# Local attention: the high and low parts of the values side by side in one operand

## The chip, the cores and the metric

The kernel runs on one core of a Trainium2 chip. The metric is the time of one execution on the device in microseconds (us); a version is told by the median of several executions. One execution of each version was also taken by the hardware profiler. The engines of the core are PE (matrix products; PEld is its loading of weights), DVE (vector engine), ACT (scalar engine), POOL (a further engine for elementwise work) and SP, which here issues the transfers (DMA).

## The reference, cut to what matters

The whole is one layer of a hybrid encoder on 1024 tokens of 1024 features, in single precision: a mixer in which windowed softmax attention and a gated DeltaNet run side by side, a cross-attention into 256 memory tokens, and a SwiGLU network. The change touches the last step of the windowed attention (8 query heads in 2 groups, 64 features a head, windows of 128 queries that see up to 384 keys):

```python
def _window_attention(q, k, v, sink):
    ...
    p = jnp.exp(scores - m)
    denom = jnp.sum(p, axis=-1, keepdims=True) + jnp.exp(sk - m)
    o = jnp.einsum('bnhgqk,bnkhd->bnqhgd', p / denom, vw)
    return o.reshape(b, s, ATTN_WIDTH)
```

## The kernel before

PE takes its operands as a short form of float32 (fp32r in the profile). To keep the precision, the kernel writes an operand as a high part, the rounded value, and a low part, what is left (the helper `split`: a copy on ACT at line 102, a subtraction on DVE at line 103). A product of two such operands is taken as three: high by high, high by low and low by high, added up in one PSUM bank.

The attention works in 16 windows: 8 blocks of 128 tokens by 2 groups of heads. `window(n, g)` is a generator with one `yield`. Its first half loads keys (`kr`, line 610), queries (`qr`, line 611) and values (`vr`, line 613), splits them, takes the scores (line 633) and the softmax (lines 635 to 650). Its second half turns the softmax weights of each block of 128 keys by four transposes on PE (line 656), splits them into `ph` and `pl`, and multiplies them by the values (line 661) into the one PSUM tile `po` (named `pow` in the profile, one buffer). There are 3 blocks in a window, 2 at the two ends of the sequence: 44 blocks in all. The values have only 64 features, so the kernel writes each of them twice side by side (`v2`), which fills the 128 columns of the weights and gives the same sums in both halves of the partitions of `po`. Two copies on ACT (lines 664 and 665) take the even heads from the lower half and the odd ones from the upper half into `ao` (one buffer), and a transfer (line 666) stores it in `d_mix`, where the output projection (`mid_gemm`, line 991) reads it later.

`next_windows` starts a window and then finishes the one started before. The written order (`ORDER_2`, `ORDER_3`) mixes these calls with the projections of queries, the levels of the DeltaNet's triangular inverses (lines 569 and 575), the scan of the DeltaNet (line 763, with updates on DVE at lines 784 and 804) and the projections of the memory tokens (lines 891 and 907). The order in which each engine gets its instructions, the queue of SP with its transfers among them, is then set by a scheduler that works from a timeline of its own, so a change in one place can move instructions in others. Each engine works its instructions off in that order.

Of the kernel before, what the change touches and what calls it, by code (L numbers as in the profile page):

```python
# [10 lines left out]
F32 = mybir.dt.float32  # L11
F32R = mybir.dt.float32r
I32 = mybir.dt.int32
AF = mybir.ActivationFunctionType
ALU = mybir.AluOpType
# [4 lines left out]
P = 128  # L20
# [55 lines left out]
def tile_hybrid_block(  # L76
# [6 lines left out]
    nc = tc.nc  # L83
# [9 lines left out]
    def f32(ap):  # L93
        return ap.bitcast(F32)

    def bc(ap, axis, shape):
        return ap.unsqueeze(axis).to_broadcast(list(shape))

    def split(hi, lo, src, scale=None, eng=None):

        if scale is None:
            nc.scalar.copy(hi, src)  # L102
            (eng or nc.vector).tensor_tensor(lo, src, f32(hi), ALU.subtract)  # L103
        else:
            nc.scalar.activation(hi, src, AF.Identity, scale=scale)
            nc.vector.scalar_tensor_tensor(lo, src, scale, f32(hi), ALU.mult, ALU.subtract)

    def pool(name, bufs, **kw):
        return tc.tile_pool(name=name, bufs=bufs, reuse_waits="tile", **kw)
# [73 lines left out]
    d_mix = dram.tile([D, S], F32, name="d_mix")  # L183
# [26 lines left out]
    for hf in range(2):  # L210
        hi = hx.tile([P, KT, HALF], F32R, name=f"hhi{hf}")
        lo = hx.tile([P, KT, HALF], F32R, name=f"hlo{hf}")
        for j in range(4):
            t = 4 * hf + j
# [95 lines left out]
    for hf in range(2):  # L310
        pp = pg.tile([P, 512], F32, tag="pg", name="pg")
        for k in range(KT):
            for a in range(2):
                nc.tensor.matmul(pp, wabr[:, k, :], hT[hf][a][:, k, :], start=(k == 0 and a == 0),
                                 stop=(k == KT - 1 and a == 1))
# [282 lines left out]
    def window(n, g):  # L598

        tok = slice(n * P, (n + 1) * P)  # L600
        k0, k1 = max(n - 1, 0), min(n + 1, NT - 1) + 1
        nb = k1 - k0
        w = nb * P
        band = C[:, _AT["band0"] - C0 + (k0 - n + 1) * P:][:, 0:w]


        kr = tw.tile([P, 384], F32, tag="kr", name="kr", bufs=1)[:, 0:w]
        qr = tw.tile([P, 4, P], F32, tag="qr", name="qr", bufs=1)
        for r in range(2):
            nc.sync.dma_start(kr[64 * r:64 * r + 64], d_k[64 * g:64 * g + 64, k0 * P:k1 * P])  # L610
            nc.sync.dma_start(qr[64 * r:64 * r + 64], d_q[256 * g:256 * g + 256, tok].rearrange("(h e) t -> e h t", h=4))
        vr = tw.tile([P, 3, 64], F32, tag="vr", name="vr", bufs=1)[:, 0:nb]
        nc.sync.dma_start(vr, d_v[k0:k1, :, 64 * g:64 * g + 64].rearrange("c p e -> p c e"))
        khi = tw.tile([P, 384], F32R, tag="khi", name="khi")[:, 0:w]
        klo = tw.tile([P, 384], F32R, tag="klo", name="klo", bufs=1)[:, 0:w]
        nc.scalar.copy(khi, kr)
        nc.gpsimd.tensor_tensor(klo, kr, f32(khi), ALU.subtract)
        vhi = tw.tile([P, 3, 2, 64], F32R, tag="vhi", name="vhi")[:, 0:nb]
        vlo = tw.tile([P, 3, 2, 64], F32R, tag="vlo", name="vlo")[:, 0:nb]
        v2 = bc(vr, 2, (P, nb, 2, 64))  # L620
        nc.scalar.copy(vhi, v2)
        nc.gpsimd.tensor_tensor(vlo, v2, f32(vhi), ALU.subtract)
        qs = tw.tile([P, 4, P], F32R, tag="qs", name="qs")
        nc.scalar.copy(qs, qr)
        nc.gpsimd.tensor_tensor(qs[64:128], qr[64:128], f32(qs[64:128]), ALU.subtract)

        m4 = tw.tile([P, 4], F32, tag="m4", name="m4")
        ssum = tw.tile([P, 4], F32, tag="ssum", name="ssum")
        pr = []
        for hh in range(4):  # L630
            pp = pw.tile([P, 512], F32, tag="pw", name="psw")
            for i, kk in enumerate((khi, klo)):
                nc.tensor.matmul(pp[:, 0:w], qs[:, hh, :], kk, start=(i == 0), stop=(i == 1))
            sc = tw.tile([P, 384], F32, tag="sc", name="sc", bufs=8)
            nc.vector.tensor_tensor_reduce(out=sc[:, 0:w], in0=pp[:, 0:w], in1=band, scale=0.125,
                                           scalar=sink[:, 4 * g + hh:4 * g + hh + 1], op0=ALU.add, op1=ALU.max,
                                           accum_out=m4[:, hh:hh + 1])
            pr.append(sc)
        nm = tw.tile([P, 4], F32, tag="nm", name="nm")
        nc.vector.tensor_scalar(nm, m4, -1.0, None, ALU.mult)  # L640
        for hh in range(4):
            nc.scalar.activation(pr[hh][:, 0:w], pr[hh][:, 0:w], AF.Exp, bias=nm[:, hh:hh + 1],
                                 accum_out=ssum[:, hh:hh + 1])
        es = tw.tile([P, 4], F32, tag="es", name="es")
        nc.gpsimd.tensor_tensor(es, sink[:, 4 * g:4 * g + 4], m4, ALU.subtract)
        nc.scalar.activation(es, es, AF.Exp)
        nc.vector.tensor_tensor(es, es, ssum, ALU.add)
        nc.vector.reciprocal(es, es)
        for hh in range(4):
            nc.scalar.mul(pr[hh][:, 0:w], pr[hh][:, 0:w], es[:, hh:hh + 1])  # L650
        yield
        po = pw.tile([P, 4, P], F32, tag="pow", name="pow", bufs=1)
        for j in range(nb):
            pp = pw.tile([P, 512], F32, tag="pw", name="ptw")
            for hh in range(4):
                nc.tensor.transpose(pp[:, hh * P:(hh + 1) * P], pr[hh][:, j * P:(j + 1) * P], ident)
            ph = tw.tile([P, 512], F32R, tag="ph", name="ph")
            pl = tw.tile([P, 512], F32R, tag="pl", name="pl")
            split(ph, pl, pp)
            for i, (vv, pe_) in enumerate(((vhi, ph), (vhi, pl), (vlo, ph))):  # L660
                nc.tensor.matmul(po.rearrange("p h t -> p (h t)"), vv[:, j].rearrange("p r e -> p (r e)"), pe_,
                                 start=(j == 0 and i == 0), stop=(j == nb - 1 and i == 2))
        ao = tw.tile([P, 2, P], F32, tag="ao", name="ao", bufs=1)
        nc.scalar.copy(ao[0:64], po[0:64, 0:4:2, :])
        nc.scalar.copy(ao[64:128], po[64:128, 1:4:2, :])
        nc.sync.dma_start(d_mix[g * 256:(g + 1) * 256, tok].rearrange("(k p) t -> p k t", p=P), ao)

    def next_windows():

        for _ in range(2):  # L670
            last = wins[-1] if wins else None
            if wins_done[0] < 2 * NT:
                wins.append(window(wins_done[0] % NT, wins_done[0] // NT))
                next(wins[-1])
            wins_done[0] += 1
            if last:
                next(last, None)
# [20 lines left out]
    tw = p12.enter_context(pool("tw", 2))  # L698
# [621 lines left out]
    for t in range(NT):  # L1320
        tok = slice(t * P, (t + 1) * P)
# [58 lines left out]
```

## Time and profile before

| what | before |
|---|---|
| median of 3 executions | 1625.35 us (1624.68 to 1629.03) |
| the profiled execution | 1627.8 us, its span 1626.1 us |
| mean granted clock of PE | 0.984 |
| PE busy, share of the span | 96% |
| weight loads busy | 80% |
| DVE, ACT, POOL busy | 58%, 46%, 33% |
| the windows' products (line 661) | from 380 to 615 us, 132 matmuls |

A busy share is the share of the span in which the engine worked on at least one instruction; matmuls overlap in it. The time of a group of instructions (busy us, mean ns of one) is followed by the idle time of its engine just before them and what ended it. The chain that ended last is followed back from the last instruction, at each step to what released it. Times within the span count from its first instruction.

### The profile page before, as it was taken

How to read it: one execution, taken by the hardware profiler on the slowest of the kernel's cores; microseconds unless marked ns; L12 is line 12 of the kernel's file. 1: busy time of each engine (PE TensorE's matmuls, PEld its weight loads, DVE VectorE, ACT ScalarE, POOL GpSimd, SP SyncE). 2: the span in 40 equal slices, each digit the busy share in tenths (PEclk: the TensorE clock that was granted, in tenths of full speed). 3: DMA queues.
4: the chain of work that ended last, by engine and by line, in shares of the span. 5: the costliest groups of instructions: out<-in, count | busy, mean ns of one | idle time of the engine just before them, and what ended most of it. 6: DMA issues, size and time to landing. Idle time of an engine off the chain costs nothing.

```text
span 1626.1 us, 21448 instructions
## 1 busy us (share of the span) xinstructions
PE 1554.1 (96%) x7690; PEld 1298.7 (80%) x7690; DVE 940.8 (58%) x1431; ACT 747.7 (46%) x1518; POOL 543.8 (33%) x501
## 2 busy tenths in 40 slices
PE   6999889999899989999999999999999999999997
PEld 5878778888799868788888777788888888888886
DVE  6855986957677864543356467666545544334332
ACT  5556553236858774564436574233233222444211
POOL 2467653334336600253202221343334332321100
PEclk9999999897999999999999999999999999999999
DMA  6134158574999585354223264432322223565451
GB/s 202 41 117 129 46 176 221 140 179 124 312 300 278 179 278 183 130 194 156 66 65 117 90 199 132 130 117 80 95 79 78 89 93 119 197 220 176 141 178 71
DMA packets 267815, 240.47 MB, mean 148 GB/s; under 512 B 43176, under 2 KB 216637, under 8 KB 267709
## 3 DMA queue, kind: packets, MB, share of 16 engines
q1 hardware_dynamic: 267709, 239.11, 47.2%
q8 instruction: 60, 0.98, 0.2%
q14 instruction: 46, 0.38, 0.1%
HBM read 177.69 MB, written 58.75 MB: 145 GB/s over the span
## 4 chain that ended last, share of the span: by engine, by line
PE 67%; DVE 10%; DMA 6%; issue 3%; ACT 3%; POOL 1%; SPq 1%; POOLq 0%; ACTq 0%; DVEq 0%
PE pmg L991 10%; PE pd L1334 8%; PE pd L1310 7%; PE pE L1163 6%; PE pD L1163 6%; PE pA L1163 6%; PE pcq L260 5%; PE pB L1163 3%; PE psc L763 3%; PE pg L260 3%; DVE acc L285 1%; DVE A L512 1%; PE pcs L1072 1%; DVE tmpb L510 1%; PE pco L1098 1%
## 5 line engine op out<-in xcount | busy, mean ns | idle before, releaser
L102 ACT CAST whi<-wraw 128x1024 fp32r<-128x1024 f32 x108 | 113.3, 1050 | 153.7 <-issue 60.0
L103 POOL TENSOR_TENSOR wlo<-wraw,whi 128x1024 fp32r<-128x1024 f32 x48 | 117.9, 2457 | 165.2 <-ACT whi L102 138.2
L260 PE MATMUL pg<-hhi,whi 128*128 128x512 f32 x352 | 143.0, 407 | 0.0
L260 PE MATMUL pg<-hlo,whi 128*128 128x512 f32 x352 | 142.3, 405 | 0.0
L260 PE MATMUL pg<-hhi,wlo 128*128 128x512 f32 x352 | 142.2, 404 | 0.0
L103 DVE TENSOR_TENSOR wlo<-wraw,whi 128x1024 fp32r<-128x1024 f32 x60 | 74.5, 1243 | 82.6 <-ACT whi L102 77.5
L991 PE MATMUL pmg<-whi,b 128*128 128x512 f32 x384 | 118.4, 395 | 2.6 <-ACT whi L102 2.2
L1163 PE MATMUL pA<-s,whi 128*128 128x512 f32 x352 | 109.5, 392 | 1.4 <-ACT m L1180 1.4
L285 DVE SCALAR_TENSOR_TENSOR acc<-cp,cols,acc 128x1024 f32<-128x1024 f32 x48 | 76.0, 1586 | 34.1 <-ACT acc L283 33.5
L991 PEld LDWEIGHTS pmg<-whi,b 128*128 128x128 f32 x384 | 71.2, 188 | 17.9 <-ACT whi L102 2.7
L1240 POOL TENSOR_TENSOR act<-act,up 128x512 f32<-128x512 f32 x33 | 44.3, 1345 | 112.3 <-issue 59.0
L260 PEld LDWEIGHTS pg<-hhi,whi 128*128 128x128 f32 x352 | 68.6, 195 | 13.6 <-ACT hhi L102 0.3
L260 PEld LDWEIGHTS pg<-hhi,wlo 128*128 128x128 f32 x352 | 68.4, 194 | 13.7
L260 PEld LDWEIGHTS pg<-hlo,whi 128*128 128x128 f32 x352 | 68.2, 194 | 13.5
L1163 PEld LDWEIGHTS pA<-s,whi 128*128 128x128 f32 x352 | 65.3, 188 | 15.1 <-ACT m L1180 2.0
L991 PE MATMUL pmg<-wlo,b 128*128 128x512 f32 x192 | 71.4, 392 | 0.0
L1212 POOL TENSOR_TENSOR sr<-wraw 128x512 f32<-128x512 f32 x22 | 28.4, 1291 | 124.8 <-DMA wraw<-in_w_gate_up_dram 118.1
L1163 PE MATMUL pA<-s,wlo 128*128 128x512 f32 x176 | 68.8, 392 | 1.1 <-DVE wlo L103 1.1
L1334 PE MATMUL pd<-wdh,ath 128*128 128x512 f32 x176 | 69.5, 395 | 0.0
L1334 PE MATMUL pd<-wdl,ath 128*128 128x512 f32 x176 | 69.5, 395 | 0.0
L1334 PE MATMUL pd<-wdh,atl 128*128 128x512 f32 x176 | 69.5, 395 | 0.0
L1310 PE MATMUL pd<-dl,whi 128*128 128x512 f32 x176 | 68.5, 389 | 0.0
(387 smaller groups left out, 4177.3 us busy)
## 6 DMA issues: line engine op xcount, KB each, us to landing
wraw<-in_w_gate_up_dram SPq DMA_DIRECT2D x52, 512.0 KB, 4.1
kv<-d_kv SPq DMA_DIRECT2D x32, 512.0 KB, 6.7
wraw<-in_w_in_dram SPq DMA_DIRECT2D x22, 512.0 KB, 4.1
araw<-d_act SPq DMA_DIRECT2D x22, 512.0 KB, 3.3
draw<-in_w_down_dram SPq DMA_DIRECT2D x22, 512.0 KB, 4.7
atr<-d_act SPq DMA_DIRECT2D x16, 704.0 KB, 4.7
d_act<-act SPq DMA_DIRECT2D x40, 256.0 KB, 2.5
d_kv<-kv SPq DMA_DIRECT2D x8, 1024.0 KB, 6.2
```

The costliest lines, as they stand in the source:

```text
L102: nc.scalar.copy(hi, src)
L103: (eng or nc.vector).tensor_tensor(lo, src, f32(hi), ALU.subtract)
L260: nc.tensor.matmul(p_, w[:, k, :], ah[a][:, k, :], start=(k == 0 and i == 0), stop=(k == nk - 1 and i == 2))
L285: nc.vector.scalar_tensor_tensor(acc, cp[:, t:t + S], taps[t], acc, ALU.mult, ALU.add)
L510: nc.vector.tensor_tensor(tv, A[:, j + 1:, j:j + 1].to_broadcast([P, n, j]), A[:, j:j + 1, 0:j].to_broadcast([P, n, j]), ALU.mult)
L763: nc.tensor.matmul(out[:, d, h, :], lt[:, d, h, :], rt[:, d, h, :], start=True, stop=True)
L991: nc.tensor.matmul(pp[t], act[a][:, k, tt], w_[:, kk, :], start=(k == 0 and i == 0), stop=(k == KT - 1 and i == 2))
L1163: nc.tensor.matmul(out_, w[a][:, k, :], xx[b_][:, k, :], start=(start and k == 0 and i == 0), stop=(k == HK - 1 and i == 2), skip_group_ch ...
L1212: nc.gpsimd.tensor_tensor(s[0], b_[:, 0:HK], b_[:, HK:], ALU.add)
L1240: nc.gpsimd.tensor_tensor(o_, o_, up, ALU.mult)
L1310: nc.tensor.matmul(pps[t], a[:, tt], b_, start=(f == 0 and i == 0), stop=(f == NF - 1 and i == 2))
L1334: nc.tensor.matmul(pp, a[:, f - f0], b_[:, f], start=(f == 0 and i == 0), stop=(f == NF - 1 and i == 2))
```

## The change

The low part of the values takes the place of their second copy. One tile `vhl` holds, for each block of keys, 64 columns of the high part and 64 of the low part, and is the weight operand of two products, by `ph` and by `pl`. The lower half of the partitions of `po` then holds the sums with the high parts and the upper half those with the low parts (the product of the two low parts comes in with them). At the end of a window the upper half is copied to `ao` by ACT, for all four heads, and DVE adds the lower half to it; the copy is written twice in the code, the same both times. `ao` has 64 partitions with four heads in place of 128 with two, and the store is written to match.

```diff
-        vhi = tw.tile([P, 3, 2, 64], F32R, tag="vhi", name="vhi")[:, 0:nb]
-        vlo = tw.tile([P, 3, 2, 64], F32R, tag="vlo", name="vlo")[:, 0:nb]
-        v2 = bc(vr, 2, (P, nb, 2, 64))
-        nc.scalar.copy(vhi, v2)
-        nc.gpsimd.tensor_tensor(vlo, v2, f32(vhi), ALU.subtract)
+
+        vhl = tw.tile([P, 3, 2, 64], F32R, tag="vhl", name="vhl")[:, 0:nb]
+        nc.scalar.copy(vhl[:, :, 0], vr)
+        nc.gpsimd.tensor_tensor(vhl[:, :, 1], vr, f32(vhl[:, :, 0]), ALU.subtract)
...
-            for i, (vv, pe_) in enumerate(((vhi, ph), (vhi, pl), (vlo, ph))):
-                nc.tensor.matmul(po.rearrange("p h t -> p (h t)"), vv[:, j].rearrange("p r e -> p (r e)"), pe_,
-                                 start=(j == 0 and i == 0), stop=(j == nb - 1 and i == 2))
-        ao = tw.tile([P, 2, P], F32, tag="ao", name="ao", bufs=1)
-        nc.scalar.copy(ao[0:64], po[0:64, 0:4:2, :])
-        nc.scalar.copy(ao[64:128], po[64:128, 1:4:2, :])
-        nc.sync.dma_start(d_mix[g * 256:(g + 1) * 256, tok].rearrange("(k p) t -> p k t", p=P), ao)
+            for i, pe_ in enumerate((ph, pl)):
+                nc.tensor.matmul(po.rearrange("p h t -> p (h t)"), vhl[:, j].rearrange("p r e -> p (r e)"), pe_,
+                                 start=(j == 0 and i == 0), stop=(j == nb - 1 and i == 1))
+        ao = tw.tile([P, 4, P], F32, tag="ao", name="ao", bufs=1)[0:64]
+        nc.scalar.copy(ao, po[64:128])
+        nc.scalar.copy(ao, po[64:128])
+        nc.vector.tensor_tensor(ao, po[0:64], ao, ALU.add)
+        nc.sync.dma_start(d_mix[g * 256:(g + 1) * 256, tok].rearrange("(h e) t -> e h t", e=64), ao)
```

## The prediction

> **What bounds the kernel now.** I read the page first, then the busy times of the stretch in which the windows of the local attention run, then the groups of instructions there, the waits, and last the chain of waits piece by piece.
>
> ```profile
> span 1626.1 us, 21448 instructions
> PE 1554.1 (96%) x7690; PEld 1298.7 (80%) x7690; DVE 940.8 (58%) x1431; ACT 747.7 (46%) x1518; POOL 543.8 (33%) x501
> ...
> PE 67%; DVE 10%; DMA 6%; issue 3%; ACT 3%; POOL 1%; SPq 1%; POOLq 0%; ACTq 0%; DVEq 0%
> ```
>
> The matrix engine PE is busy 96% of the span and carries 67% of the chain that ended last, so time taken from PE is worth most where nothing else waits. The next rows cut the stretch of the windows into four parts (length, then busy time of PE, weight loads, DVE, ACT, POOL with counts, granted clock, DMA share, GB/s).
>
> ```profile
> 380.00:420.00 40.00, 34.71 (x156) 29.20 (x157) 25.34 (x60) 27.86 (x71) 16.14 (x18) 0.70 0.56 168
> 420.00:540.00 120.00, 113.28 (x888) 107.68 (x887) 89.81 (x250) 84.80 (x228) 58.79 (x59) 1.00 0.97 303
> 540.00:580.00 40.00, 37.85 (x256) 33.76 (x255) 30.89 (x66) 32.67 (x100) 19.55 (x25) 1.00 0.54 154
> 580.00:620.00 40.00, 35.07 (x165) 27.64 (x164) 23.95 (x34) 29.98 (x51) 0.90 (x2) 1.00 0.86 292
> ```
>
> From 420 to 580 us PE is busy 151 of 160 us at full clock, DVE 121 (75%) and ACT 117 (73%). From 380 to 420 us the granted clock is 0.70, so something other than PE sets the pace there; from 420 to 540 us the DMA engines are 0.97 busy as well. The chain pieces (start, length, what) show where PE's work is what counts and where it is not:
>
> ```profile
> 416.37 9.60 DMA kv<-d_kv
> 426.05 7.33 DMA wraw<-in_w_ckv_dram
> ...
> 436.34 0.70 PE pow L661 x3
> ...
> 442.32 0.69 PE pow L661 x3
> ...
> 464.54 4.26 SPq L610
> 468.85 5.23 DMA kr<-d_k
> ...
> 580.61 10.54 DMA wraw<-in_w_ckv_dram
> ```
>
> **What the change removes.** Of the three products per block of 128 keys (high values by high weights, high by low, low by high) one goes. These are the groups of line 661, first for 380 to 620 us, then its last row again for the parts 380 to 420, 420 to 580 and 580 to 620 us (count, then busy us and mean ns).
>
> ```profile
> L661 PE MATMUL pow<-pl,vhi 128*128 128x512 f32 x44 | 21.2, 481 | 3.6 <-DVE pl L103 3.5
> L661 PE MATMUL pow<-ph,vhi 128*128 128x512 f32 x44 | 20.9, 476 | 10.9 <-ACT ph L102 10.4 <-ACT ao L665 0.4
> L661 PE MATMUL pow<-ph,vlo 128*128 128x512 f32 x44 | 18.3, 415 | 0.0
> L661 PEld LDWEIGHTS pow<-ph,vlo 128*128 128x128 f32 x44 | 9.0, 205 | 0.5
> L661 PE MATMUL pow<-ph,vlo 128*128 128x512 f32 x8 | 4.1, 511 | 0.0
> L661 PE MATMUL pow<-ph,vlo 128*128 128x512 f32 x28 | 11.0, 394 | 0.0
> L661 PE MATMUL pow<-ph,vlo 128*128 128x512 f32 x8 | 3.2, 394 | 0.0
> ```
>
> 44 matmuls go, and with them 44 weight loads. What is one worth? Its row says 415 ns, but matmuls overlap: in the chain three of them take 0.69 us (442.32), so one costs 0.23 us of issue. The price of the whole is 44 x 0.23 = 10.1 us, not the 18.3 us of the row. The Trainium skill, "Perfetto Trace Analysis", section Identifying the Most-Contended Engine, says that matmul busy time misleads because the instructions are pipelined, and that weight-load time is the better measure; by that the removed work is the 9.0 us of the weight-load row, so the sum would be 1.1 us smaller. The trace bears the rule out, 0.23 us in the chain against 415 ns in the group.
>
> How much of the 10.1 us counts? 28 of the 44 lie between 420 and 580 us, where PE is nearly always at work: 28 x 0.23 = 6.4 us, taken in full. Eight lie after 580 us: 8 x 0.23 = 1.8 us, of which I take 0.9, since the chain there runs 10.54 us through a weight transfer that no matmul hastens, and PE is busy only 35.07 of 40 us. Eight lie before 420 us, at a clock of 0.70, ahead of the 9.60 us transfer of kv: at most 8 x 0.23 / 0.70 = 2.6 us, and I take 0, because the next stage starts with that transfer. Together 7.3 us, with ends of 0 and 10.8 us (6.4 + 1.8 + 2.6).
>
> **What it adds and moves.** The rows of the same stretch that price it:
>
> ```profile
> L102 ACT CAST ph<-ptw 128x512 fp32r<-128x512 f32 x44 | 25.5, 583 | 2.8 <-PE ptw L656 2.3
> L664 ACT COPY ao<-pow 64x256 f32<-64x256 f32 x16 | 5.8, 362 | 11.5 <-DMA d_mix<-ao 6.9 <-PE pow L661 4.6
> L665 ACT COPY ao<-pow 64x256 f32<-64x256 f32 x16 | 5.9, 367 | 0.2
> L621 ACT CAST vhi<-vr 128x384 fp32r<-128x384 f32 (+1 forms) x14 | 6.8, 487 | 8.3 <-PE pow L661 8.2
> L622 POOL TENSOR_TENSOR vlo<-vr,vhi 128x384 fp32r<-128x384 f32 (+1 forms) x14 | 13.7, 982 | 66.4 <-ACT vhi L621 38.2 <-PE psw L633 15.8 <-PE pck L891 7.4
> L817 DVE TENSOR_TENSOR ol<-ol,psc 128x512 f32<-128x512 f32 x8 | 5.4, 680 | 0.1
> ```
>
> ACT: each of the 16 windows had two copies of 64 x 256 (0.362 + 0.367 us). Now it has two copies of 64 x 512; the diff writes the same copy twice, and the second one adds nothing but time. No copy of that shape is in the trace. Its bounds are 0.365 us, if the length of a row did not count, and 0.583 us, the cast of 512 elements out of the same memory; I take 0.58, because length is what differs between these rows. That is 16 x (1.16 - 0.73) = 6.9 us more. The cast of the values shrinks from 384 to 192 elements a row: from 0.487 to between 0.36 (the 256-element copy) and about 0.30, so 16 x 0.14 = 2.2 us less. ACT gains 4.7 us of work.
>
> DVE: a new addition of 64 x 512 per window, one operand in PSUM, as the 0.680 us of line 817: 16 x 0.68 = 10.9 us more. POOL: the subtraction for the low part halves, 16 x about 0.45 = 7 us less, and worth nothing: POOL sat idle 66.4 us before these very instructions.
>
> What is queued behind this? The tail of a window is last product, copy, copy, addition, store; it takes 2 x 0.58 + 0.68 = 1.84 us in place of 0.73. In the built order the next window's first product into the same PSUM bank stands 4 us of PE work or more behind the last one, once 2 us (estimated at 0.23 us for a product of 512), so the bank is free in time when ACT and DVE are prompt. On ACT the two copies hold up the casts of the transposed weights (ph), and on DVE the addition holds up pl and the scan's own updates. These are the waits of PE that stand there already, and those of the store:
>
> ```profile
> PE pow L661 <- ACT ph L102: 10.4, 8, 2.2
> PE pow L661 <- DVE pl L103: 3.5, 6, 1.1
> ...
> SPq L666 <- ACT ao L665: 15.3, 9, 5.1
> ```
>
> 13.9 us of waiting for 345 us of ACT and DVE work between 380 and 620 us (sums of the four parts) is 4%; by that the 15.6 us added would cost 0.6 us. Work added where an engine is three quarters full costs more than the mean, so I take 2.0 us, with ends of 0 and 15.6. The store of ao moves behind the addition; the queue of SP waited 15.3 us for ao before. In the built order the store now stands behind loads (of vr, d_q, kr) that used to follow it, so these don't wait longer for it; I cost it at 0, and at 16 x 1.1 = 18 us if every window's loads waited. The store's shape changes from 128 partitions of two rows to 64 of four, each run still 128 floats: 0. The built order also differs over the whole stretch and a little in later ones; I cost that at 0 with 4 us to either side, an estimate from the single holes of 4 to 5 us (464.54, 468.85) that one load in another place makes or mends.
>
> Sum: -7.3 + 2.0 = -5.3 us. The profiled execution took 1627.8 us (span 1626.1), so it would be 1622.5; the median of before is 2.45 us below that execution, so the forecast is 1625.35 - 5.3 = **1620.0 us**. What a measurement of this kernel can tell from no change is about 0.3%, 4.9 us; the forecast lies just beyond.
>
> **Rivals.**
> (a) All the PE time comes back and the added work hides. For it: PE is the chain for 67%. Against it: the clock of 0.70 and the two long transfers. Time 1625.35 - 10.1 = 1615.2; chance 0.08.
> (b) The DMA engines set the pace from 420 to 540 us, so PE merely waits for kv, pz and weights in place of multiplying. For it: share 0.97 and 303 GB/s; chain pieces of DMA of 5 to 10 us. Against it: 113.28 of 120 us of PE busy. Then only what lies after 540 us counts, about a quarter of the 6.4 us plus 0.9: -2.5 us, with the 2.0 us added 1625; chance 0.27.
> (c) Slower: the tail of the window becomes the bound. ACT and DVE take their queues in order; if ph and pl of the next window stand right behind the two copies and the addition, each window lengthens by the 1.84 - 0.73 = 1.1 us of tail. In all 16 windows that is 17.8 us, less the 7.3 us that count: +10.5; in two thirds of them +4.5. It decides from the point at which PE's wait for ph and pl, 13.9 us now, passes 21.2 us (13.9 + 7.3). For it: PE holes of 2.2 us before ph exist now. Time 1630 to 1636, 1632 for one number; chance 0.22.
> (d) The clock. In the profile 380 to 420 us ran at 0.70 while PE was busy 34.71 of 40 us, and 420 to 540 us at 1.00 with 113.28 of 120. If fewer matmuls make PE sparse enough for the lower clock in 20 us more, that costs 20 x 0.30 = 6 us and the gain is gone: 1626. Against it: the longest hole of the dense part is short.
>
> ```profile
> 492.99 0.50 PE L661 MATMUL pow<-ph,vhi 128*128 128x512 f32 x1 [2.19 <-ACT ph L102]
> ```
>
> Chance 0.05. The Trainium skill, "TensorE: Matmul & The Clock Gate", section What's actually happening, states that the clock halves after an idle window of about 3.4 us; a hole of 2.19 us is shorter, so by that rule too the clock should stay.
> (e) The change not doing what it says can be left out: the built order holds two products per block.
>
> **Numbers.** Forecast 0.38 and (a) 0.08 are faster, though near the bound of 4.9 us: part of the forecast's mass (0.04) falls inside it, so faster is 0.42. (b), (d) and that part give 0.36 for no change, (c) 0.22 for slower. The range reaches from 1611 (the 10.1 us and 4 us of better order) to 1635 (rival (c) with 3 us of worse order).
>
> **What would show it.** Right: 88 matmuls on pow, three quarters of their gain in 420 to 580 us, the last window's store some 5 us earlier, copies of about 0.58 us and additions of 0.68, PE's waits for ph and pl under 18 us together. Wrong: scan and windows ending no earlier with more DMA pieces in the chain (b); waits of PE for ph, pl or the new ao above 21.2 us (c); a clock under 1.00 after 420 us (d); copies of 0.37 us or an addition far from 0.68 would upset the price.

## The result, and the profile after

The changed kernel takes 1632.41 us (median of 6 runs, 1632.21 to 1637.4) where the kernel before takes 1627.19 us on the same chip. The ratio is 1.0039 with a 95% interval of 1.0021 to 1.0057: slower by 6.3 us (3.4 to 9.3; here and below microseconds are the ratio less one, times 1628; the two medians themselves lie 5.2 us apart). The forecast was 1620.0 us, faster by 5.3.

First the page of the changed kernel: span, busy times, and shares of the chain that ended last.

```profile
span 1630.5 us, 21375 instructions
...
PE 1545.3 (95%) x7646; PEld 1290.9 (79%) x7646; DVE 945.5 (58%) x1447; ACT 751.5 (46%) x1518; POOL 538.3 (33%) x501
...
PE 62%; DVE 9%; DMA 5%; ACT 4%; issue 3%; POOL 1%; SPq 1%; POOLq 0%; ACTq 0%; DVEq 0%
```

PE has 44 matmuls fewer and is busy 8.8 us less (1554.1 before), yet the span is 4.4 us longer. PE's share of the chain fell from 67 to 62%, so time that was PE's work became waiting. The same four stretches as in the prediction (length, busy time of PE, weight loads, DVE, ACT, POOL, granted clock, DMA share, GB/s) show where:

```profile
380.00:420.00 40.00, 31.79 (x171) 26.50 (x172) 29.52 (x75) 32.66 (x83) 15.41 (x20) 0.83 0.63 191
420.00:540.00 120.00, 111.73 (x878) 106.05 (x878) 94.40 (x252) 84.68 (x221) 55.97 (x59) 1.00 0.95 299
540.00:580.00 40.00, 32.95 (x198) 29.32 (x197) 24.62 (x55) 28.01 (x84) 16.36 (x20) 0.91 0.49 140
580.00:620.00 40.00, 34.47 (x157) 26.74 (x156) 25.35 (x43) 31.84 (x59) 2.96 (x5) 0.96 0.75 253
```

From 540 to 580 us every engine is less busy than before (PE 32.95 for 37.85, DVE 24.62 for 30.89, ACT 28.01 for 32.67): something is waited for in turn, and no engine is full. Up to there the changed kernel was ahead: the scan's 493rd product (psc, line 763) starts at 531.0 us where it started at 536.6. Of this lead 2.7 us stand already at the scan's first product (413.7 for 416.3 us), a place that varies from 412.3 to 418.9 us over the profiles of all kernels here. The scan's last product (line 843) starts at 570.6, before at 570.2. So 5.6 us of lead are gone in 40 us. The merge's first product then starts 2.3 us late (611.6 for 609.3), and the transposes behind it 4.3 us late (682.6 for 678.3); from there the distance no longer changes much. The store of the last window, forecast some 5 us earlier, is issued at 628.2 us where it was at 615.8.

The chain pieces of that stretch (start, length, what) show the turn-taking:

```profile
547.71 1.00 POOL klo L617
548.72 0.48 SPq L610
...
549.25 4.56 DMA kr<-d_k
...
553.89 0.47 ACT khi L616
...
554.92 1.98 ACT sc L641 x7
556.90 0.48 ACT vn L793
...
557.42 3.20 PE psc L763 x16
```

The buffer of the keys (`kr`) comes free when POOL has taken the low part of the last keys (`klo`); only then is the next load issued, and it takes 4.56 us. ACT stands at the cast of those keys, and behind it in ACT's queue are the exponentials and a copy for the scan (`vn`), on which PE waits. From 420 to 580 us as a whole ACT stands no longer for the keys than before (13.1 us for 14.0), so this place is an example and not the account.

The groups of the changed lines, 380 to 620 us as in the prediction (count, busy us, mean ns, then idle time of the engine before them and what ended it):

```profile
L660 PE MATMUL pow<-ph,vhl 128*128 128x512 f32 x42 | 19.6, 466 | 5.8 <-ACT ph L102 4.7 <-DVE ao L665 1.2
L660 PE MATMUL pow<-pl,vhl 128*128 128x512 f32 x42 | 19.1, 455 | 1.7 <-DVE pl L103 1.5
L665 DVE TENSOR_TENSOR ao<-pow,ao 64x512 f32<-64x512 f32 x14 | 9.5, 678 | 4.6 <-ACT ao L664 4.6
L663 ACT COPY ao<-pow 64x512 f32<-64x512 f32 x15 | 8.7, 582 | 9.7 <-PE pow L660 6.1 <-DMA d_mix<-ao 3.2
L664 ACT COPY ao<-pow 64x512 f32<-64x512 f32 x15 | 8.7, 581 | 0.1
L620 ACT CAST vhl<-vr 128x192 fp32r<-128x192 f32 x11 | 3.9, 352 | 0.0
```

The prices of the prediction for ACT and DVE are there: copies of 0.582 and 0.581 us (0.58 forecast), the addition 0.678 (0.68), the cast 0.352 (0.30 to 0.36). Only POOL's subtraction, forecast about 0.45 us shorter, went from 0.982 to 0.635 us; it was given no worth. PE's waits for `ph`, `pl` and the bank of `ao` are 4.7 + 1.5 + 1.2 = 7.4 us, less than before (14.3).

### The profile page after: what moved, and what is told of

Read it like the earlier page. It is cut to its first block, busy times and chain, and to the rows that moved or that the text cites. A ratio compares the mean times of both kernels' runs of the same rounds, so it can differ in the third digit from the quotient of the medians.

```text
span 1630.5 us, 21375 instructions
## 1 busy us (share of the span) xinstructions
PE 1545.3 (95%) x7646; PEld 1290.9 (79%) x7646; DVE 945.5 (58%) x1447; ACT 751.5 (46%) x1518; POOL 538.3 (33%) x501
## 4 chain that ended last, share of the span: by engine, by line
PE 62%; DVE 9%; DMA 5%; ACT 4%; issue 3%; POOL 1%; SPq 1%; POOLq 0%; ACTq 0%; DVEq 0%
PE pmg L991 10%; PE pd L1334 8%; PE pd L1310 7%; PE pE L1163 6%; PE pD L1163 6%; PE pA L1163 6%; PE pcq L260 5%; PE pB L1163 3%; PE psc L763 2%; PE pcs L1072 1%; PE pco L1098 1%; DMA wraw<-in_w_gate_up_dram 1%; PE pg L260 1%; DVE wlo L103 1%; PE pow L660 1%
```

## The experiments

The change did three things at once: fewer products, a longer window end, and another order of instructions on every engine, since the scheduler draws it anew. To part them, some kernels keep a recorded order. Every instruction is tied to its predecessor on its engine:

```python
for a, b in zip(order, order[1:]):
    tc.add_manual_dep(per[e][b], per[e][a].name, ...)   # an order, no wait
```

"Old order" is that of the kernel before, "new order" that of the changed kernel. An addition that the old order lacks stands where its copy had ended; a third product that the new order lacks stands right behind the second. No run ties the kernel before to its own order and changes nothing else; the nearest one, with a second buffer for the keys (at the end of this section), took 1.6 us less than the kernel before, so the tying shows no price of its own.

**New work in the old order; old work in the new order.** No other edit.

> The changed kernel's instructions, but each engine gets them in the order that the kernel before had (two products in the places of the first two of three, the copies and the store in the old places, the new addition on DVE at the first place after the second copy). Theory 'order' (the re-drawn order of the whole stretch is what costs, the work itself saves): 4 to 9 us below before, as the forecast's sum of -5.3 us had it. Rival 'tail' (the copies on ACT and the addition on DVE cost more than the products save): 3 to 8 us above before, as the change itself was.

> The instructions of the kernel before (three products, two short copies, no addition), but each engine gets them in the order of the changed kernel, the third product right behind the second. Theory 'order': slower than the changed kernel, by the 5 to 10 us of PE work that come back, so 10 to 15 us above before. Rival 'tail': at or below before, 0 to 6 us, since the costly tail is gone.

New work, old order: 1639.35 us, ratio 1.0069 (1.0051 to 1.0088), +11.2 us. Old work, new order: 1632.7 us, 1.0024 (1.0008 to 1.004), +3.9 us. So the order alone costs something, but the changed work is dearer still in the old order; the theory that only the order did harm fell. The rival 'tail' has the sign of the first but not its size (3 to 8 us), and the second lies between what the two theories gave.

**The copy once**, in the old order and in an order drawn freely:

```diff
-        nc.scalar.copy(ao, po[64:128])
         nc.scalar.copy(ao, po[64:128])
```

> As the first one, with the copy to ao written once. 16 copies of 0.58 us go from ACT, 9.3 us of work. Theory 'order': 0 to 3 us below the first one, since little of ACT's work lies on the path. Rival 'tail': 4 to 9 us below it.

> The changed kernel with the copy to ao written once, the order left to the scheduler. Rival 'tail': 4 to 9 us below the changed kernel, 3 us above to 4 below before. Theory 'order': this is one more draw of the order, so its distance from the third one, which does the same work in the old order, is what the order is worth here: at least 3 us either way.

Old order: 1.0039 (1.0023 to 1.0055), +6.3 us, 4.9 below the one with two copies. Free order: 1.0025 (1.0007 to 1.0044), +4.1 us, 2.2 below the changed kernel, too little to tell. The second copy is a part of the price, but not the whole.

**Products and window end apart**, in both orders. Two kernels have two products and the old end, two have three products and the new end.

```diff
 # two products, old end
-        nc.scalar.copy(ao, po[64:128])
-        nc.scalar.copy(ao, po[64:128])
-        nc.vector.tensor_tensor(ao, po[0:64], ao, ALU.add)
+        nc.scalar.copy(ao[0:64], po[0:64, 0:4:2, :])
+        nc.scalar.copy(ao[64:128], po[64:128, 1:4:2, :])
...
```

> Two products per block and the one operand of high and low values, but the window's end as before (two copies of 64x256, no addition; the sums with the low parts are not added, and the odd heads take them). Every engine keeps before's order. It stands against the new work in the old order, which took 11 us more than before. Theory 'tail' (the products' time comes back, the two copies and the addition cost more than that): without the tail the products show, 5 to 10 us under before. Theory 'clock and holes' (PE's freed time turns into holes and into stretches at half the clock, so the products are worth nothing): within 3 us of before, with more lost clock after 420 us than before.

> Three products per block as before, and the changed window's end (copy, the same copy again, addition, store of 64 partitions; the attention result comes out doubled). Before's order on every engine. Theory 'tail': the tail alone costs 14 to 21 us, so 1642 to 1649. Theory 'clock and holes': the tail costs what the whole new work cost in this order, 8 to 12 us, so 1636 to 1640, at a clock no lower than before's.

> As the first of these four, but in the order of the changed kernel. It stands against the old work in that order (before + 3.9 us). Theory 'tail': 5 to 10 us under that, so 1623 to 1628. Theory 'clock and holes': within 3 us of it.

> As the second of these four, but in the order of the changed kernel (the attention result comes out doubled). It stands against the changed kernel itself and the old work in this order. Theory 'tail': 5 to 10 us over the changed kernel, 1637 to 1643. Theory 'clock and holes': within 3 us of the changed kernel, with fewer windows at half the clock than it has, since PE is denser.

With the runs above this makes all eight combinations (us against the kernel before):

| | old order | new order |
|---|---|---|
| three products, old end | 0 | +3.9 (1.3 to 6.5) |
| two products, old end | -1.3 (-4.7 to 2.1) | +2.3 (-0.5 to 5.0) |
| three products, new end | +11.7 (7.0 to 16.4) | +8.5 (5.5 to 11.6) |
| two products, new end | +11.2 (8.3 to 14.3) | +6.3 (3.4 to 9.3) |

Down the columns: taking the products away is worth 1.3 and 0.5 us in the old order, 1.6 and 2.2 in the new one, 1.4 in the mean, not 7.3. The new end costs 11.7 and 12.5 us in the old order, 4.6 and 4.0 in the new one, not 2.0. Each single difference is uncertain by 3 to 6 us and the mean of the four by about 2, so the 1.4 can't be told from nothing, but it is clearly under the 6.4 us that the prediction took in full. Both theories were half right: the products bring nearly nothing and the end costs more than they could bring.

One caution: the 12 executions with two products, old end and old order fall into two groups of six (1621.5 to 1626.0 and 1631.4 to 1637.1 us). The profiled one took 1637.1 us, so its rows below are of the second group.

**A fourth product** (low values by low weights), old end, old order:

```diff
-            for i, (vv, pe_) in enumerate(((vhi, ph), (vhi, pl), (vlo, ph))):
+            for i, (vv, pe_) in enumerate(((vhi, ph), (vhi, pl), (vlo, ph), (vlo, pl))):
...
```

> The kernel before with a fourth product per block (low values by low weights, 44 more matmuls of 512 columns, 44 x 0.23 = 10.1 us of issue), before's order on every engine, before's window end. Theory 'PE sets the pace' (as the prediction counted: 28 x 0.23 in full): 6 to 10 us slower than before, 1636 to 1640. Theory 'holes and clock' (PE's time between the products and the casts is slack, so a product more or less is nearly free): 0 to 3 us slower, no more lost clock than before.

1634.86 us, 1.0041 (1.0024 to 1.0058), +6.7 us. So a product more costs about what PE's issue says (28 x 0.23 = 6.4), and a product less gives almost nothing back. Waits of the weight loads of line 661 (660 with two products) from 420 to 580 us (us, times, longest); four products, then three (the kernel before), then two:

```profile
PEld pow L661 <- ACT ph L102: 4.9, 4, 2.1
PEld pow L661 <- DVE pl L103: 1.9, 5, 0.7
```

```profile
PEld pow L661 <- ACT ph L102: 6.8, 5, 2.4
PEld pow L661 <- DVE pl L103: 3.6, 6, 1.3
```

```profile
PEld pow L660 <- ACT ph L102: 10.6, 6, 3.3
PEld pow L660 <- DVE pl L103: 3.8, 6, 1.1
```

6.8, 10.4 and 14.4 us: each product taken away adds about 4 us of waiting for `ph` and `pl`. This wait alone doesn't explain the difference between the two steps, since from four products to three it grows as much, and there the time was saved. What only the second step shows is a lower clock. The same three kernels from the scan's first product to the merge's first (columns as in the four stretches):

```profile
415.33:611.05 195.72, 186.32 (x1305) 170.25 (x1305) 139.35 (x347) 144.66 (x376) 79.85 (x87) 0.99 0.86 269
```

```profile
416.33:609.31 192.98, 179.17 (x1268) 163.63 (x1269) 139.86 (x347) 143.32 (x376) 80.24 (x87) 0.99 0.87 273
```

```profile
418.93:614.39 195.46, 176.40 (x1233) 161.61 (x1234) 139.16 (x347) 141.87 (x376) 75.59 (x87) 0.96 0.86 269
```

PE idles 9.4, 13.8 and 19.1 us, and the granted clock is 0.99, 0.99 and 0.96. The clocks of all executions agree, not only those of the profiled ones: 0.985 in the mean with four products and 0.985 with three beside it, but 0.984 with three and 0.982 with two (old end), and 0.983 and 0.980 (new end), all in the old order. In a time of 1630 us, 0.002 of clock are 3 us of PE at full speed. In the new order the clock falls by 0.001 only, and the products bring no more. So the saving went into idle time of PE and, in the old order, a lower clock; how much each of them takes was not isolated.

**The copies without the addition** (three products, old order):

```diff
-        nc.vector.tensor_tensor(ao, po[0:64], ao, ALU.add)
```

> The three products and the changed window's end without its addition (two copies of 64x512 on ACT, store of the second), before's order. It stands against the same kernel with the addition (1638.5, 11.7 us over the kernel before, if both kernels before are set equal). Theory 'copies' (ACT's queue holds ph back): the copies cost 8 to 12 us, so 1637 to 1641 and the addition nearly nothing. Theory 'addition' (DVE's 0.68 us holds pl and the scan back): the copies cost 2 to 6 us, so 1631 to 1635, the addition the rest.

1633.83 us, 1.0034 (1.0018 to 1.005), +5.5 us. Of the 11.7 us of the new end in this order the longer copies are 5.5 and the addition 6.2. That lies in the range of the theory 'addition', near its end; with 2.9 to 8.1 us for the copies the two theories can't be told apart by this run.

**Two buffers for the keys**, order free, with the work before and with the changed work with one copy:

```diff
-        kr = tw.tile([P, 384], F32, tag="kr", name="kr", bufs=1)[:, 0:w]
+        kr = tw.tile([P, 384], F32, tag="kr", name="kr", bufs=2)[:, 0:w]
```

> The kernel before with two buffers in place of one for the keys' load (kr), everything else, and the order, free. Theory 'head of queue' (ACT stands at the cast of the keys until the load lands, 14.6 us in the profile of before): 4 to 10 us faster than before. Theory 'order' (what is moved by the scheduler decides more than any single wait): between 5 us faster and 5 us slower, without a drop that matches the wait.

> The changed kernel with the copy once and two buffers for the keys' load, order free: the candidate to beat both. Theory 'head of queue': 6 to 10 us under the changed kernel, about level with before or a little under. Theory 'order': within 4 us of the changed kernel with one copy (before + 4.1 us).

Before with two buffers: 1.0032 (1.0015 to 1.0048), +5.2 us. One copy with two buffers: 1.0019 (1.0006 to 1.0033), +3.1 us. The theory of the head of the queue fell. But the profiles tell something more: the second kernel starts the scan's last products at 562.8 us, 7.4 us before the kernel before does, and the transposes behind the merge at 677.8, only 0.5 us earlier. Its chain between (start, length, what):

```profile
620.92 3.70 DMA d_mix<-ao
624.68 5.04 DMA b<-d_mix
...
631.97 0.69 DVE z L994
632.71 19.12 PE pmg L990 x83
```

The last window's store and its reload stand in front of the steps (`z`) that empty the merge's banks; whether they cost the lead is tried further down, in another kernel.

**The waiting products moved back.** In the old order, wherever PE waited over 0.4 us for `ph` or `pl` between 405 and 600 us, the product goes behind as many later PE instructions as fill the wait. Only the order of PE changes. The second kernel has two products and the old end, the third the changed work with one copy.

> The kernel before, every engine in its own order, but at the 11 places between 405 and 600 us where PE waited over 0.4 us for ph or pl (12.3 us together) the waiting product goes behind as many PE instructions as fill the wait (3 to 11 of them). Theory 'cover' (PE stands at the head of its queue although other work is ready): 4 to 9 us faster than before, 1618 to 1623. Theory 'second bound' (scan, casts or transfers run at the same pace, so PE then waits for them): within 3 us of before, with PE's waits for the scan's operands in place of those for ph and pl.

> The same for the kernel with two products and the old window end (the sums with the low parts are not added): at 14 places its products go behind the PE instructions that fill their waits (18.7 us together). Theory 'cover': with the waits filled the removed products are worth what PE's issue says, so 5 to 8 us under the run before it in this list, 1612 to 1617. Theory 'second bound': within 3 us of that run.

> The changed work with the copy once, in before's order, its products moved back at 13 places in the same way (15.6 us of waits): the candidate to beat both. Without the moves it took before + 6.4 us. Theory 'cover': 6 to 10 us under that, level with before or a little under, 1622 to 1627. Theory 'second bound': before + 3 to + 6.

They took 1.003 (1.0016 to 1.0045), 1.0052 (1.0033 to 1.0072) and 1.0095 (1.0074 to 1.0116): +4.9, +8.5 and +15.5 us, all slower than without the moves. The theory that PE only stood badly at the head of its queue fell clearly; the ranges of the 'second bound' (3, 3 and 6 us at most) were passed too. The second kernel is 3.6 us over the first, so the products are worth nothing here either. PE's weight loads stand no less in the first kernel than before, 12.7 us for 13.0 from 420 to 580 us, now for other work, the scan's and the transposes' above all, and the granted clock there is 0.98 for 1.00. ACT's waits in the same time; before, then three products moved back, then two:

```profile
ACT khi L616 <- DMA kr<-d_k: 14.0, 6, 4.7
...
ACT vhi L621 <- PE pow L661: 3.8, 3, 3.2
```

```profile
ACT vhi L621 <- PE pow L661: 8.4, 4, 3.9
ACT khi L616 <- DMA kr<-d_k: 7.3, 4, 4.4
```

```profile
ACT vhl L620 <- PE pow L660: 14.8, 4, 6.2
ACT khi L616 <- DMA kr<-d_k: 11.8, 4, 5.4
```

ACT has to cast the next window's values, whose buffer comes free with the products; it now stands for PE 8.4 and 14.8 us where it stood 3.8 (and 3.5 with two products not moved). So ACT and PE can wait for each other in a ring: `ph` from ACT, products on PE, the buffer back to ACT. That the ring makes the price is not shown: in the first kernel ACT's wait for the keys fell by more than its wait for PE grew.

**z ahead of the casts.** Three products, new end, old order; on ACT and DVE the first three steps of lines 994 and 995 go ahead of the last casts of the reloaded result.

> Three products and the new window end in before's order (before + 11.7 us), with one thing moved: on ACT and DVE the first three steps that empty the merge's sums (lines 994 and 995 of before) go ahead of the last casts of the reloaded attention result (b), which stand waiting for the last windows' store. Theory 'merge' (a part of the tail's price in the old order is this wait, 2.37 us of PE and a stretch at half the clock behind it): 2 to 4 us under the same kernel without the move, before + 7 to + 10. Rival (the tail's price lies in the windows alone): within 1.5 us of it, before + 11 to + 13.

1640.59 us, 1.0067 (1.0048 to 1.0086), +10.9 us beside +11.7: no difference that can be told, as the rival had it. PE's waits for the merge from 600 to 700 us, without and with the move:

```profile
PEld pmg L991 <- DVE z L995: 2.8, 1, 2.8
PEld pmg L991 <- ACT whi L102: 2.7, 1, 2.7
```

```profile
PEld pmg L991 <- ACT whi L102: 4.5, 2, 2.7
...
PEld pmg L991 <- DVE wlo L103: 1.1, 1, 1.1
```

5.5 us before, 5.6 after: the wait for `z` turned into one for the next weights.

**Two key buffers in the old order**, with the work before, and with the changed work with one copy and three buffers for the values' operand.

> The kernel before, every engine in its own order, with two buffers in place of one for the keys' load (kr). It differs from the earlier run with two key buffers only in that the order is kept. Theory 'loop' (what sets the pace of a window is the chain load of keys, cast of keys on ACT, exponentials, cast of ph, products, cast of the next values, in which ACT stands 14.0 us for the keys between 420 and 580 us): the wait falls under 7 us and the time by 3 to 8 us, 1619 to 1625 if before is 1627. Rival (the load then waits for the next thing in SP's queue): ACT's wait for keys stays over 10 us and the time within 2 us of before.

> The changed work with the copy once, in before's order (before + 6.4 us), with two key buffers and three buffers for the values' operand, which the narrower operand leaves room for. Theory 'loop': both waits of ACT (15.8 us for keys, 5.4 us for the values' operand with the copy twice) fall by half or more, and the time by 5 to 10 us, before - 4 to + 1. Rival: before + 4 to + 8.

0.999 (0.9972 to 1.0007), -1.6 us, and 1.0031 (1.0016 to 1.0046), +5.0 us: the rival holds in both. ACT still waits for the keys in the first one, and SP shows why; 420 to 580 us, first the run with two buffers (its profile is of the longest of its 12 executions), then the kernel before:

```profile
ACT khi L616 <- DMA kr<-d_k: 13.0, 3, 6.1
```

```profile
SPq L666 <- ACT ao L665: 12.9, 4, 5.2
```

```profile
SPq L666 <- ACT ao L665: 9.1, 4, 5.1
```

A free buffer doesn't bring the load forward: SP stands at the store of `ao` until ACT has copied it, and what follows in SP's queue, loads of keys among it, stands behind. No version tried beats the kernel before by more than the runs can tell.

## Why the prediction was wrong, point by point

**The products: 28 x 0.23 = 6.4 us taken in full, 7.3 in all.** This is the first step that failed; it measured 1.4 us. The price of 0.23 fits the fourth product (+6.7 us), and the count was right (88 matmuls left). Wrong was to read "PE busy 151 of 160 us" as "PE sets the pace", so that all time taken from PE would come off the span. In its place the runs show PE idle for longer, 5.3 us more with two products than with three (13.8 to 19.1 us in the profiles, old end and order), and in the old order a lower clock besides. Filling the waits for `ph` and `pl` with other PE work made the kernels slower. Why a fourth product costs its issue time, though PE's idle time shrinks with it by 4.4 us, while the third brings nothing back, stays open in part: the clock is the one difference that the record shows. A slope measured on one side, a product more, does not hold on the other.

**The tail: 2.0 of 15.6 us.** The second step that failed; it measured 4.3 us in the new order and 12.1 in the old one. The ratio of waits to work (4%) was the wrong guide. The upper end of the prediction, 15.6, was nearer the truth in the old order than the value taken. PE's waits for `ph` and `pl` did not grow with the new end, and that the merge behind the windows makes the difference was tried and not borne out. What follows the price is a term that the prediction put at 0, the store of `ao` at the head of SP's queue. In the old order SP stands there until `ao` is done, and what it issues next, the values' loads among it, stands behind; in the new order the store comes later in the queue. SP's waits at the store (line 666, or 667 in kernels with three products and the new end), 380 to 620 us, all rows added up (us):

| | old order | new order |
|---|---|---|
| three products, old end | 19.3 | 3.2 |
| two products, old end | 18.1 | 6.3 |
| three products, new end | 34.9 | 8.7 |
| two products, new end | 33.1 | 9.0 |

The longest of these rows; three products, new end, old order, then the same in the new order, then old work in the new order:

```profile
SPq L667 <- DVE ao L666: 15.8, 6, 4.2
SPq L667 <- DVE m L635: 9.2, 3, 6.7
```

```profile
SPq L667 <- DVE kv L784: 4.0, 2, 3.4
```

```profile
SPq L666 <- ACT ao L665: 1.0, 1, 1.0
```

The new end lengthens this wait by 15.6 and 15.0 us in the old order and by 5.5 and 2.7 in the new one, where it costs 11.7 and 12.5, and 4.6 and 4.0; the copies without the addition lengthen it by 8.8 (to 28.1) and cost 5.5. So the prediction was right that in the built order the store holds up little, and in the old order its bound of 18 us for this term was the better number. It is a match of sizes and not a proof: no run moved the store in SP's queue, and on PE the price isn't seen in one wait (ACT's wait for the keys is 14.6 us before and 14.2 with three products, new end, old order).

**The re-drawn order: 0 with 4 us to either side.** It measured +3.9 us, at the edge of that. The place seen is the load of keys behind POOL's `klo` at 548.72 us. That this one place is the whole of the 3.9 is not shown, and two buffers for the keys brought nothing.

Together 3.9 + 4.6 - 2.2 = 6.3 us, one path through the table of eight.

**The rivals.** The measured 1632.41 us is almost the number of rival (c), 1632, and its cause, copies and addition in the window end, is the largest single term (4.0 to 4.6 us, beside 3.9 for the order). That the number fits is luck, for the 6.3 us also hold the price of the order, which (c) did not have. And its sign in the profile was not there: PE's waits for `ph`, `pl` and `ao` came to 7.4 us where (c) asked for over 21.2, because in the new order PE waits elsewhere (2.54 us for `vn` before 557.42 us). With the new work in the old order they came to 17.0 us (11.9, 3.4 and 1.7), and with three products and the new end, which alone cost 11.7 us, to 13.0, less than the 14.3 of before. So the end's price is not paid where (c) put it, and the point from which (c) was to decide was never reached. The prediction's own sign, waits for `ph` and `pl` under 18 us, came true (6.2 us) while the time went the other way, so these waits were the wrong thing to watch. Rival (b), no gain for the products since transfers set the pace, was right on the gain and is not shown as the cause: the DMA share of 420 to 540 us is 0.95 to 0.97 with and without the change.

**Rival (d), the clock,** was given 0.05 because the longest hole was short. It did fall: 0.91 and 0.96 in the two parts after 540 us, 1.00 before, which is 0.09 x 40 + 0.04 x 40 = 5.2 us of PE at full speed. Old work in the new order shows it too (0.97 over 420 to 580 us), so there it comes with the order. In the old order it falls with the products, as (d) had it: from 0.984 to 0.982 and from 0.983 to 0.980 in the mean of all executions, some 3 and 5 us of PE at full speed. So 0.05 was too little for (d). How much of the time it makes by itself was not isolated.

## What to carry to other kernels

A busy engine is not a bound until work added and work taken away both move the time; if only the first does, look where the saving went, into waits or into a lower clock. Work at the end of a step, on which a store waits, is not to be priced by how busy its engine is: here that gave 2.0 us, and the runs 4 to 12. Look how long the queue that issues the store already stands at it. When a scheduler draws the order anew, run the new work in the old order and the old work in the new one before any of it is explained.

## What the runs showed of the hardware that was not expected

The granted clock halves for stretches of 3.4 us though PE was not idle before them. Windows of 3.4 us of the changed kernel (columns as above):

```profile
544.50:547.90 3.40, 1.76 (x9) 1.26 (x9) 3.01 (x5) 2.98 (x7) 3.23 (x5) 0.99 0.44 106
547.90:551.30 3.40, 3.14 (x15) 3.14 (x16) 2.61 (x9) 0.58 (x1) 3.24 (x5) 0.50 0.22 59
551.30:554.70 3.40, 3.40 (x28) 3.09 (x27) 2.26 (x4) 0.81 (x3) 0.97 (x1) 1.00 0.74 229
554.70:558.10 3.40, 0.86 (x8) 0.68 (x7) 1.45 (x7) 3.40 (x13) 0.00 (x0) 1.00 0.29 84
558.10:561.50 3.40, 3.40 (x19) 3.40 (x18) 1.17 (x2) 2.96 (x11) 1.20 (x2) 0.50 0.00 0
```

After 1.76 and after 0.86 us of PE work in 3.4 us the next stretch runs at 0.50, and after 3.14 us the clock is back at 1.00. Not every such window does it: in the kernel before, on the grid of its own clock changes, 1.60 us of PE work in 3.4 us was followed by full clock:

```profile
563.50:566.90 3.40, 1.60 (x10) 1.24 (x10) 3.04 (x4) 3.40 (x13) 0.91 (x2) 1.00 0.14 42
566.90:570.30 3.40, 3.08 (x15) 2.30 (x16) 3.03 (x8) 3.40 (x11) 1.20 (x2) 1.00 0.84 231
```

The prediction's rule of a whole idle window (the Trainium skill, "TensorE: Matmul & The Clock Gate", section What's actually happening) is too mild for this trace: at these two places a window about half empty, or emptier, was enough. The length of the stretches, 3.4 us, agrees with that page. The longest holes in those two windows are these:

```profile
547.07 0.50 PE L660 MATMUL pow<-ph,vhl 128*128 128x512 f32 x1 [1.27 <-ACT ph L102]
...
557.42 1.49 PE L763 MATMUL psc<-vn,pz 128*128 128x128 f32 x8 [2.54 <-ACT vn L793]
```

Holes of 1.27 and 2.54 us, both shorter than an idle window, were followed by 3.4 us at half the clock, 1.7 us of PE's work each.
